# An encoder block on one core: later modulation columns with the weights as the moving operand, and loads for weight sums placed behind the raw weights of their step

## The chip, the cores and the metric

The kernel runs on one core of one Trainium2 chip. The metric is the device time of an execution in microseconds; lower is better.

## The reference

One encoder layer serves two request groups, a prompt of 2048 tokens and a sample of 512, with 1024 channels. A conditioning vector per group gives six vectors of 1024 numbers that modulate the layer. All is float32.

```python
mod = silu(c) @ w_ada + b_ada              # w_ada: 1024 x 6144, c: 2 rows in all
shift1, scale1, gate1, shift2, scale2, gate2 = split(mod, 6)
h = rmsnorm(x, g_mix_norm) * (1 + scale1) + shift1
z = h @ w_in
y_f = fourier_mixer(z[..., :512])          # 2-D DFT, then per-head maps
y_s = s5_mixer(z[..., 512:])               # bidirectional state space, GELU, GLU
x = x + gate1 * (concat(rmsnorm(y_f), rmsnorm(y_s)) @ w_out)
h = rmsnorm(x, g_mlp_norm) * (1 + scale2) + shift2
ff = square(relu(h @ w_mlp_in + b_mlp_in)) @ w_mlp_out + b_mlp_out
return rmsnorm(x + gate2 * ff, g_final)
```

## The kernel before

Activations lie with channels on the partitions and tokens along the free dimension. The modulation vectors are kept the same way, as `mod`, 128 partitions by 48 columns by 2 groups: column j holds 128 of the 6144 numbers. Products that need more than one pass are split: each operand into a high part (a cast, `wh`, `th`) on ScalarE and a low part (the rest, `wl`) on VectorE, and `mm3` (lines 229 to 231) issues three matmuls, high by high, high by low, low by high.

The stages in order of time: the input projection with the first sixteen modulation columns (`ada1`, line 705: the two conditioning rows stationary, 512 weight columns moving, then four small transposes at line 710); a stage from about 345 to 690 us in which blocks of the state-space scan (`psV` at L350, `psY` at L382), the Fourier mixer (`px`, `pyc`, `pys`) and its output (`pof`) share TensorE with the 32 later modulation columns; the gated units and the output projection (`pgate`, `pval`, `pout`), to about 1020 us; and the MLP.

The later columns: `ada(j)` (line 681) multiplies one 128-column piece of `w_ada` in eight matmuls. The weights are stationary, the two columns of `cs` (the activated conditioning) move, and the result has channels on partitions; VectorE adds the bias (L688). `ada_slot` calls it once in each of 32 slots between pieces of the scan. Its weights, 512 KB a column, are loaded on the SP queue into two buffers named `wa` (`AB = 2`): the load for column j+2 is issued behind the matmuls of column j, whose buffer it takes.

The MLP works by a scheme with seven products for eight, so it needs sums of weight quarters. `precombine` (line 1247) makes a sixteenth of one weight's sums: four loads of 256 KB on SP (L1258), four additions on GpSimd (L1263), four stores of 256 KB on ScalarE's DMA queue (L1264) to a scratch in DRAM, `wS`. Twenty of the 32 pieces are made beside the output projection; the last twelve, all for the second MLP weight, are made in the first 60 steps of the MLP, in a buffer (`big4`) that those steps don't need yet, with room for three pieces at a time. A step is twelve matmuls against 128 x 512 weights. Two steps share a load of raw weights (`wr`, L1394), and in the first third of the MLP the low parts are also stored for later (`wL`, L1408). The first block's input is scaled by VectorE and ScalarE (`h2`, L1324 and L1325) before its first product.

The order on every engine is set by the scheduler of the framework, which places instructions by a model of time; each engine and each DMA queue then runs its own in that order. `tc.issue_after(ins)` makes the instructions of a block that run on the engine of `ins` come behind it there.

Of the kernel before, what the change touches and what calls it, by code (L numbers as in the profile page):

```python
# [26 lines left out]
AB = 2  # L27
# [532 lines left out]
class Net:  # L560
# [3 lines left out]
    def run(self):  # L564
        tc, nc, A = self.tc, self.nc, self.A
        with ExitStack() as es:
            self.cp = es.enter_context(tc.tile_pool(name="cp", bufs=1))
            dp = self.dp = es.enter_context(tc.tile_pool(name="dp", bufs=1, space=DRAM))
            self.pst, self.side = None, False
            self.pr = es.enter_context(tc.tile_pool(name="psr", bufs=1, space=PSUM))  # L570
            self.banks(7)
            es.callback(lambda: self.pst.close())
            self.uD = dp.tile([512, 8, 320], F32, name="uD")
            self.yD = dp.tile([512, 8, 320], F32, name="yD")
            self.fD = dp.tile([4, 128, NT], F32, name="fD")
            nb = 32 // NQ
            self.sD = [dp.tile([nb, 128] + sh + [NQ, 128], F32, name="s%d" % i) for i, sh in enumerate(([2], [2], []))]
            self.sD.append(dp.tile([nb, 128, 3, NQ, 40], F32, name="s3"))
            self.zD = dp.tile([4, 5, 128, 258], F32, name="zD")
            self.pD = dp.tile([8, 128, NT], F32, name="pD")  # L580
            self.rD = dp.tile([128, NT], F32, name="rD")
            self.x1D = dp.tile([8, 128, NT], F32, name="x1D")
            self.wS = [dp.tile([4, 8, 128, 1024], F32, name="wS%d" % i) for i in range(2)]

            self.wL = dp.tile([112, 128, 1024], F32, name="wL")
            self.consts()
            def pool(name, side=None):
                st = ExitStack()
                return st, st.enter_context(tc.tile_pool(name=name, bufs=1, side=side))
            spps, spp = pool("spp", "right")  # L590
            fes, fe = pool("fe", "right")
            self.Ze = [fe.tile([96, n], F32R, name="Ze%d" % n) for n in (352, 256)]
            self.aj, self.wa = 16, {}
            self.pcs = [(w, c) for w in range(2) for c in range(16)]
            P = self.mix_in(spp)
            sas, sa = pool("ssa", "right")
            sps, sp = pool("ssm", "right")
            S = Ssm(self, P, sa, sp, self.uD.rearrange("(g h) t n -> (h t) g n", g=32), self.yD.rearrange("(g h) t n -> (h t) g n", g=32), *self.sD)
            self.ada_open(sa, 48)
            gen = self.beside()  # L600
            self.pull(gen, U0)
            bl = []
            for q in range(nb + 2):
                if q < nb:
                    bl.append(S.lead(q))
                    self.slot(gen)
                if 1 <= q <= nb:
                    S.step2(bl[q - 1])
                if q >= 2:
                    self.slot(gen)  # L610
                    S.step3(bl[q - 2])
                    self.slot(gen)
                if q < nb:
                    S.step1(bl[q])
                    self.slot(gen)
            self.pull(gen, 1000)
            self.banks(7)
            sps.close()
            sas.close()
            fes.close()  # L620
            spps.close()
            xb = es.enter_context(tc.tile_pool(name="xb", bufs=1))
            self.x0 = xb.tile([128, 16, 428], F32, name="x0")
            self.mws = es
            self.mix_out()
            self.mlp()
# [53 lines left out]

    def ada(self, j):
        nc = self.nc
        v3 = lambda n: self.v[n].unsqueeze(2).broadcast_to([128, 8, 2])
        ps = self.ps([128, 2], "pa")
        w = self.wa.pop(j)
        for k in range(8):
            nc.tensor.matmul(ps, w[:, k], self.cs[:, k], start=k == 0, stop=k == 7)  # L687
        nc.vector.tensor_scalar(self.mod[:, j], ps, self.v["b_ada"][:, j:j + 1], None, op0=ALU.add)  # L688
        if j == 39:
            nc.vector.scalar_tensor_tensor(self.gs2, self.mod[:, 32:40], 1.0, v3("g_mlp_norm"), op0=ALU.add, op1=ALU.mult)  # L690
        if j == 47:
            nc.vector.tensor_scalar(self.ng2, self.mod[:, 40:48], -1.0, None, op0=ALU.mult)
            nc.vector.tensor_tensor(self.gb2, self.mod[:, 40:48], v3("b_mlp_out"), op=ALU.mult)
# [21 lines left out]
    def ada_slot(self):  # L715
        j = self.aj
        if j < self.aend:
            self.ada(j)
            if j + AB < self.aend:
                self.ada_load(self.adp, j + AB, AB)  # L720
            self.aj += 1

    def ada_open(self, tp, end):
# [542 lines left out]
    def mlp(self):  # L1266
        tc, nc, A = self.tc, self.nc, self.A
# [11 lines left out]
        with tc.tile_pool(name="mp1", bufs=1, side="right") as t1, tc.tile_pool(name="mp", bufs=1, side="right") as tp:  # L1279
# [5 lines left out]
            def big(bl, role):  # L1285
                return ring[bl["slots"][role]][:, :, :bl["n"]]
# [100 lines left out]
            raws, los = {}, {}  # L1387
            trail = lambda st: self.wL[(st["i"] % (2 * PH)) // 2].rearrange("p (a b) -> p a b", a=2)

            def raw(i):  # L1390
                st = steps[i]
                w = A["w%d" % st["ph"]] if st["kind"] == "raw" else self.wS[st["ph"] - 1]
                raws[i] = mw.tile([128, 2, 512], F32, tag="wr", name="wr", bufs=3)
                nc.sync.dma_start(raws[i].rearrange("p a b -> p (a b)"), w[st["j"], st["m"] // 2])  # L1394
                los[i] = mw.tile([128, 2, 512], F32R, tag="wl", name="wl", bufs=3)
                if st["bl"] is not blocks[0]:
                    nc.sync.dma_start(los[i].bitcast(F32), trail(st))
# [109 lines left out]
            def pre2(c):  # L1507
                if c == 0:
                    bl = blocks[0]
                    bl["sc"] = big(bl, "21").rearrange("p a b -> p (a b)")  # L1510
                t = blocks[0]["sc"]
                self.precombine(lambda n, i: t[:, 512 * (i + 4 * (c % 3)):512 * (i + 4 * (c % 3)) + 512])
            for c in range(len(self.pcs)):
                at(P0 + (60 - P0) * c // len(self.pcs), pre2, c)
            for st in steps:
# [5 lines left out]
            for i in range(len(steps) + 24):  # L1521
                for f, a in hooks.get(i, ()):
                    f(*a)
                if i >= len(steps):
                    continue
                for j in ([0, 1, 2] if i == 0 else [i + LW]):
                    if j < len(steps):
                        if j % 2 == 0 and j not in raws:
                            raw(j)
                        weights(j)  # L1530
                if (i + 4) % 2 == 0 and i + 4 < len(steps) and i + 4 not in raws:
                    raw(i + 4)
                (mm_in if steps[i]["ph"] == 1 else mm_out)(steps[i])
# [15 lines left out]
```

## Time and profile before

| | us |
|---|---|
| median of 3 runs | 2659.03 |
| lowest and highest | 2655.82, 2665.93 |
| the profiled execution | 2665.03 |
| its span, first to last instruction | 2663.3 |
| TensorE busy | 2530.6 (95%) |
| weight loads on TensorE | 2285.1 (86%) |
| VectorE busy | 1683.9 (63%) |
| ScalarE busy | 1293.1 (49%) |
| GpSimd busy | 478.7 (18%) |
| mean granted TensorE clock | 0.954 |
| DMA moved | 627 MB, 236 GB/s in the mean |

The busy time of TensorE includes matmuls that run at the lower of its two clocks, and the profile models the ends of matmuls, so a busy engine can still be slower than it might be; the granted clock of a stretch (1 is 2.4 GHz, 0.5 is 1.2 GHz) tells how much. In the trace an f32 matmul shows as two records and one on split operands as one. A chain of waits is followed back from the last instruction to what released each step.

### The profile page before, as it was taken

The numbers are of one execution on the slowest core, as the hardware profiler recorded it, in microseconds if no ns is written. First come the engines' busy times: TensorE is split into PE (matmuls) and PEld (weight loads), VectorE is DVE, ScalarE is ACT, GpSimd is POOL, SyncE is SP. The second block draws the span as 40 slices with busy tenths as digits, with TensorE's granted clock in tenths as the row PEclk, the third lists the DMA queues.
The fourth block names the chain that finished last, engine by engine and source line by source line (L and its number), as shares of the span: only waits on it lengthen the run. The fifth ranks groups of instructions, "written<-read, shape, count | busy, mean of one in ns | idle before, by whom it ended". The sixth has DMA issues, their size and how long they took to land.

```text
span 2663.3 us, 35333 instructions
## 1 busy us (share of the span) xinstructions
PE 2530.6 (95%) x12643; PEld 2285.1 (86%) x12643; DVE 1683.9 (63%) x2775; ACT 1293.1 (49%) x2267; POOL 478.7 (18%) x406
## 2 busy tenths in 40 slices
PE   6889999999989999799999999999999999999997
PEld 2778878778767779689999999999999999999997
DVE  7888778776638866758867973354456433634454
ACT  2643466564534425525544557355445573654443
POOL 4410010000346430940400002004000020130000
PEclk8789988879999999899999999999999999999998
DMA  8644476455678978997666777676667766766664
GB/s 293 205 146 113 141 246 214 163 171 184 206 274 268 308 253 288 339 365 277 233 218 216 276 257 251 228 273 230 226 230 276 248 243 226 274 226 227 226 222 163
DMA packets 279040, 627.31 MB, mean 236 GB/s; under 512 B 66512, under 2 KB 110608, under 8 KB 277072
## 3 DMA queue, kind: packets, MB, share of 16 engines
q1 hardware_dynamic: 238416, 549.13, 60.3%
q10 hardware_dynamic: 34096, 61.32, 6.2%
q0 software_dynamic: 6352, 14.60, 1.7%
q8 instruction: 100, 1.64, 0.3%
q14 instruction: 76, 0.62, 0.1%
HBM read 469.10 MB, written 155.85 MB: 235 GB/s over the span
## 4 chain that ended last, share of the span: by engine, by line
PE 68%; DVE 12%; DMA 10%; ACT 4%; issue 4%; POOL 2%; ACTq 0%; SPq 0%; DVEq 0%; POOLq 0%
PE acc L231 9%; PE acc L230 9%; PE acc L229 9%; PE pf L231 8%; PE pf L230 8%; PE pf L229 8%; PE pa L687 2%; PE psY L382 2%; PE psV L350 1%; DMA xq<-in_xq 1%; POOL q L1263 1%; DMA wS<-q 1%; DMA q<-in_w 1%; DVE wl L1406 1%; PE pof L229 1%
## 5 line engine op out<-in xcount | busy, mean ns | idle before, releaser
L1404 ACT CAST wh<-wr 128x512 fp32r<-128x512 f32 x672 | 413.4, 620 | 689.3 <-PE acc L230 342.7
L229 PE MATMUL pf<-th,wh 128*128 128x426 f32 (+1 forms) x1344 | 483.2, 360 | 19.7 <-ACT wh L1404 19.6
L230 PE MATMUL pf<-th,wh 128*128 128x426 f32 (+1 forms) x1344 | 482.2, 359 | 1.0 <-DVE th L1357 1.0
L231 PE MATMUL pf<-th,wl 128*128 128x426 f32 (+1 forms) x1344 | 477.3, 359 | 5.2 <-DVE wl L1406 5.1
L230 PE MATMUL acc<-th,wh 128*128 128x426 f32 (+1 forms) x1344 | 478.4, 357 | 0.3 <-DVE th L1357 0.3
L229 PE MATMUL acc<-th,wh 128*128 128x426 f32 (+1 forms) x1344 | 474.5, 357 | 0.0
L231 PE MATMUL acc<-th,wl 128*128 128x426 f32 (+1 forms) x1344 | 466.9, 357 | 2.1 <-DVE wl L1406 2.0
L1424 DVE TENSOR_TENSOR big<-big,pf 128x426 f32<-128x426 f32 (+1 forms) x320 | 185.1, 596 | 237.2 <-PE pf L231 191.6
L1357 DVE TENSOR_TENSOR th<-big,th 128x1704 fp32r<-128x1704 f32 (+1 forms) x82 | 158.8, 1936 | 201.8 <-ACT th L1356 201.5
L229 PEld LDWEIGHTS pf<-th,wh 128*128 128x128 f32 x1344 | 254.3, 189 | 32.8 <-ACT wh L1404 23.4
L231 PEld LDWEIGHTS pf<-th,wl 128*128 128x128 f32 x1344 | 254.3, 189 | 18.0 <-DVE wl L1406 9.1
L230 PEld LDWEIGHTS pf<-th,wh 128*128 128x128 f32 x1344 | 254.7, 190 | 10.1 <-DVE th L1357 1.4
L231 PEld LDWEIGHTS acc<-th,wl 128*128 128x128 f32 x1344 | 253.2, 189 | 11.2 <-DVE wl L1406 2.8
L230 PEld LDWEIGHTS acc<-th,wh 128*128 128x128 f32 x1344 | 252.5, 188 | 9.5 <-DVE th L1357 1.1
L229 PEld LDWEIGHTS acc<-th,wh 128*128 128x128 f32 x1344 | 252.9, 188 | 9.0
L750 POOL TENSOR_TENSOR r<-r,mh 128x4 f32<-128x4 f32 (+3 forms) x32 | 35.3, 1109 | 1145.1 <-DVE r L749 1145.1
L1431 POOL TENSOR_TENSOR big<-big 128x426 f32<-128x426 f32 (+1 forms) x128 | 142.6, 1118 | 493.4 <-ACT big L1430 490.1
L1406 DVE TENSOR_TENSOR wl<-wr,wh 128x512 fp32r<-128x512 f32 x224 | 174.9, 799 | 62.6 <-ACT wh L1404 62.1
L1263 POOL TENSOR_TENSOR q<-q,q 128x512 f32<-128x512 f32 x80 | 138.4, 1730 | 79.6 <-DMA q<-in_w 57.4
L1356 ACT CAST th<-big 128x1704 fp32r<-128x1704 f32 (+1 forms) x82 | 132.5, 1616 | 0.7 <-PE acc L231 0.7
L1357 DVE TENSOR_TENSOR th<-x,th 128x1704 fp32r<-128x1704 f32 (+1 forms) x23 | 47.5, 2066 | 69.3 <-ACT th L1356 69.3
L1430 ACT ACTIVATE big<-big 128x426 f32<-128x426 f32 (+1 forms) x128 | 71.3, 559 | 38.7 <-DVE big L1424 35.5
(444 smaller groups left out, 4453.4 us busy)
## 6 DMA issues: line engine op xcount, KB each, us to landing
wl<-wL SPq DMA_DIRECT2D x224, 512.0 KB, 3.5
wr<-wS SPq DMA_DIRECT2D x192, 512.0 KB, 4.5
wr<-in_w SPq DMA_DIRECT2D x144, 512.0 KB, 4.4
wL<-wl SPq DMA_DIRECT2D x112, 512.0 KB, 3.4
wa<-in_w_ada SPq DMA_DIRECT2D x48, 512.0 KB, 4.7
q<-in_w SPq DMA_DIRECT2D x80, 256.0 KB, 4.3
wS<-q ACTq DMA_DIRECT2D x80, 256.0 KB, 3.7
big<-x1D SPq DMA_DIRECT2D x8, 1704.0 KB, 7.8
```

The lines of the kernel that those rows point to most:

```text
L229: nc.tensor.matmul(out, l[0], r[0], start=start, stop=False)
L230: nc.tensor.matmul(out, l[0], r[1], start=False, stop=False)
L231: nc.tensor.matmul(out, l[1], r[0], start=False, stop=stop)
L382: nc.tensor.matmul(py, m, x[:, j], start=i == 0, stop=i == 2)
L1263: e.tensor_tensor(o, x, y, op=op)
L1356: nc.scalar.copy(th[0], src)
L1357: return th, v.tensor_tensor(th[1], src, th[0].bitcast(F32), op=ALU.subtract)
L1404: nc.scalar.copy(hi, r)
L1406: v.tensor_tensor(lo, r, hi.bitcast(F32), op=ALU.subtract)
L1424: v.tensor_tensor(f[q], f[q], ps, op=op)
L1430: nc.scalar.activation(f[q], f[q], AF.Relu)
L1431: nc.gpsimd.tensor_tensor(f[q], f[q], f[q], op=ALU.mult)
```

## The change

The later columns take the form of the first sixteen: `cs` is stationary (two columns), the 128 weight columns move, and the result is a 2 x 128 row. ScalarE copies it into the front of the weights' own buffer; TensorE transposes it to 128 x 2, and VectorE adds the bias as before. The transpose and the addition of a column are issued one slot later, in `ada_turn`, behind the matmuls of the next column. Since the row lies in the weights' buffer, the buffer comes free with the transpose; the load of column j+1 is then issued in slot j, behind the transpose of column j-1. In the MLP, the loads of a weight sum are placed behind the last raw-weight load that was issued before them.

```diff
     def ada(self, j):
-        ps = self.ps([128, 2], "pa")
+        ps = self.ps([2, 128], "pa")
         w = self.wa.pop(j)
         for k in range(8):
-            nc.tensor.matmul(ps, w[:, k], self.cs[:, k], start=k == 0, stop=k == 7)
+            nc.tensor.matmul(ps, self.cs[:, k], w[:, k], start=k == 0, stop=k == 7)
+        r = w[:2, 0]
+        nc.scalar.copy(r, ps)
+        self.ada_turn()
+        self.turn = (j, r)
+
+    def ada_turn(self):
+        if not self.turn:
+            return
+        (j, r), self.turn = self.turn, None
+        ps = self.ps([128, 2], "pat")
+        nc.tensor.transpose(ps, r, self.ident[:2, :2])
         nc.vector.tensor_scalar(self.mod[:, j], ps, self.v["b_ada"][:, j:j + 1], None, op0=ALU.add)
...
             self.ada(j)
-            if j + AB < self.aend:
-                self.ada_load(self.adp, j + AB, AB)
+            if 16 < j <= self.aend - AB:
+                self.ada_load(self.adp, j + AB - 1, AB)
...
-                nc.sync.dma_start(raws[i].rearrange("p a b -> p (a b)"), w[st["j"], st["m"] // 2])
+                self.wload = nc.sync.dma_start(raws[i].rearrange("p a b -> p (a b)"), w[st["j"], st["m"] // 2])
...
-                self.precombine(lambda n, i: t[:, 512 * (i + 4 * (c % 3)):512 * (i + 4 * (c % 3)) + 512])
+                with tc.issue_after(self.wload.ins):
+                    self.precombine(lambda n, i: t[:, 512 * (i + 4 * (c % 3)):512 * (i + 4 * (c % 3)) + 512])
```

TensorE among the later columns, between the Fourier mixer and the scan's outputs, before the change (`pa` are the columns, two of them, 36 and 37, in the first row and two in the last; `psY` are the scan's outputs):

```order
L687 MATMUL pa<-cs,wa 128x2 x16
L382 MATMUL psY<-un,Th 128x320
L382 MATMUL psY<-S,O 128x320 x2
L382 MATMUL psY<-un,Th 128x320
L382 MATMUL psY<-S,O 128x320 x2
L382 MATMUL psY<-un,Th 128x320
L382 MATMUL psY<-S,O 128x320 x2
L382 MATMUL psY<-un,Th 128x320
L382 MATMUL psY<-S,O 128x320 x2
L687 MATMUL pa<-cs,wa 128x2 x16
```

and at a like place with the change (columns 32, 33 and 34; `pat` is a transpose, buffer numbers tell which weights):

```order
L687 MATMUL pa_5101<-wa_5018,cs_93 2x128 x8
L702 MATMUL pat_5111<-ident_84,wa_4947 128x2
L687 MATMUL pa_5156<-wa_5114,cs_93 2x128 x8
L702 MATMUL pat_5166<-ident_84,wa_5018 128x2
L382 MATMUL psY_5236<-un_4370,Th_4423 128x320
L382 MATMUL psY_5236<-S_5227,O_4421 128x320
...
L687 MATMUL pa_5257<-wa_5169,cs_93 2x128 x8
L702 MATMUL pat_5267<-ident_84,wa_5114 128x2
```

The eight matmuls of a column now come as one piece with a transpose of the column before behind them; `wa_5114` takes the buffer of `wa_4947`, so the second row's transpose stands directly ahead of the matmuls that need the load issued behind it.

SP's queue in the first steps of the MLP, before (`wr` raw weights, `wL` stores of low parts, `big4` the loads of sums):

```order
L1394 DMA wr_9490<-in_w1 128x1024
L1408 DMA wL_79<-wl_9416 128x1024
L1394 DMA wr_9542<-in_w1 128x1024
L1258 DMA big4_9177<-in_w2 128x512 x12
L1408 DMA wL_79<-wl_9454 128x1024
L1408 DMA wL_79<-wl_9492 128x1024
L1394 DMA wr_9580<-in_w1 128x1024
L1394 DMA wr_9638<-in_w1 128x1024
```

and with the change, beginning with the fifth raw load:

```order
L1409 DMA wr_9422<-in_w1 128x1024
L1273 DMA big4_9273<-in_w2 128x512 x4
L1423 DMA wL_79<-wl_9336 128x1024
L1409 DMA wr_9460<-in_w1 128x1024
L1273 DMA big4_9273<-in_w2 128x512 x2
L1423 DMA wL_79<-wl_9374 128x1024
L1273 DMA big4_9273<-in_w2 128x512 x2
L1409 DMA wr_9510<-in_w1 128x1024
```

The loads of sums stood twelve in a row behind the tenth raw load; now they come one piece (four loads) at a time from the fifth on.

VectorE at the entry of the MLP, before (`xo` are the output projection's additions, `x` the scaling of the MLP's input, `wl` low weights, `th` the input's low part):

```order
L1324 SCALAR_TENSOR_TENSOR x_6810<-x_6810,gs_98,rb 128x428 x14
L1229 TENSOR_TENSOR ss<-ss,sq 128x512
L1224 SCALAR_TENSOR_TENSOR xo<-pout,mod,xo 128x512
L1220 SCALAR_TENSOR_TENSOR xo<-pf,mod,xo 128x512
L1324 SCALAR_TENSOR_TENSOR x_6810<-x_6810,gs_98,rb 128x428 x2
L1406 TENSOR_TENSOR wl<-wr,wh 128x512 x4
L1220 SCALAR_TENSOR_TENSOR xo<-pf,mod,xo 128x512
L1224 SCALAR_TENSOR_TENSOR xo<-pout,mod,xo 128x512
L1357 TENSOR_TENSOR th_9179<-x_6810,th_9178 128x1712
```

and with the change:

```order
L1239 SCALAR_TENSOR_TENSOR xo<-pout,mod,xo 128x512
L1339 SCALAR_TENSOR_TENSOR x_6906<-x_6906,gs_98,rb 128x428 x15
L1244 TENSOR_TENSOR ss<-ss,sq 128x512
L1339 SCALAR_TENSOR_TENSOR x_6906<-x_6906,gs_98,rb 128x428
L1421 TENSOR_TENSOR wl<-wr,wh 128x512 x4
L764 TENSOR_SCALAR r<-pn 128x4
L1372 TENSOR_TENSOR th_9275<-x_6906,th_9274 128x1712
```

Before, several of the projection's additions stood behind the scaling; now the first row is the last of them, and the whole scaling follows.

## Rows read from the trace of the kernel before

**Rows 1.** Windows by stage: stretch and length, busy us (instructions) per engine, clock, DMA share, GB/s.

```profile
345.00:690.00 345.00, 337.91 (x1649) 276.90 (x1648) 264.18 (x695) 193.91 (x449) 11.50 (x16) 0.86 0.59 193
1020.00:1200.00 180.00, 154.90 (x753) 142.12 (x753) 113.64 (x130) 79.36 (x139) 96.24 (x66) 0.94 0.94 340
1200.00:2663.00 1463.00, 1444.76 (x7440) 1394.01 (x7439) 802.73 (x1042) 736.40 (x1131) 147.18 (x140) 0.99 0.68 239
```

**Rows 2.** Chain of waits from 345 to 690 us, shares by line.

```profile
by line: PE pa L687 12.5%; PE psY L382 12.4%; PE psV L350 9.8%; PE pof L230 5.5%; PE pof L229 5.5%; PE pof L231 5.5%; issue 4.1%; PE px L229 3.7%; PE px L231 3.6%; PE px L230 3.6%; DMA fD<-yF 3.1%; DMA raw<-in_w_out 2.3%; PE pc L999 1.6%; A
```

**Rows 3.** Timeline of TensorE: start, length in us, line, tiles, shapes, records.

```profile
345.35 6.83 PE L687 MATMUL pa<-cs,wa 128*128 128x2 f32 x32
...
616.61 1.84 PE L687 MATMUL pa<-cs,wa 128*128 128x2 f32 x16
...
627.47 1.86 PE L382 MATMUL psY<-un,Th 128*128 128x320 f32 x6
```

**Rows 4.** Windows of L687 alone, 340 to 660 us: their sum.

```profile
sum 320.00, PE 71.05 PEld 72.84; mean PE 11.84 PEld 12.14
```

**Rows 5.** Windows of 6 us, columns as in rows 1.

```profile
336.00:342.00 6.00, 2.38 (x8) 0.89 (x6) 1.29 (x4) 5.89 (x21) 4.78 (x8) 1.00 0.87 250
342.00:348.00 6.00, 5.44 (x20) 4.07 (x18) 3.70 (x9) 5.80 (x19) 0.00 (x0) 0.51 1.07 373
...
408.00:414.00 6.00, 6.00 (x32) 5.15 (x32) 5.55 (x17) 3.01 (x14) 1.50 (x3) 0.69 1.13 356
```

**Rows 6.** Timeline of TensorE among the first sixteen columns.

```profile
39.51 3.59 PE L705 MATMUL pa<-wa,cs 128*2 128x512 f32 x8
...
51.47 0.41 PE L710 MATMUL pat<-ident,ar 2*128 2x2 f32 x4 [2.27 <-ACT ar L707]
```

**Rows 7.** Windows of 4 us among the first sixteen columns, columns as in rows 1.

```profile
28.00:32.00 4.00, 4.00 (x6) 0.60 (x5) 3.50 (x26) 1.15 (x2) 0.00 (x0) 0.57 1.03 350
...
40.00:44.00 4.00, 3.10 (x8) 0.44 (x6) 3.97 (x11) 0.77 (x1) 2.91 (x2) 1.00 0.48 140
```

**Rows 8.** Tile wa, whole span: ns min/median/max, first and last start.

```profile
L705 PEld LDWEIGHTS pa<-wa,cs x64: 80/85/129, 5.7 to 48.2; 128*2 128x2 f32 x64
```

**Rows 9.** Tile wa, 340 to 660 us: its loads, issue to landing.

```profile
DMA to landing us min/median/max: 3.1/3.9/11.1
```

**Rows 10.** Windows in the first steps of the MLP, columns as in rows 1.

```profile
1170.00:1180.00 10.00, 7.92 (x40) 6.80 (x39) 7.76 (x8) 2.28 (x4) 5.82 (x5) 1.00 1.05 411
1057.00:1187.00 130.00, 105.94 (x490) 94.82 (x489) 86.05 (x86) 57.30 (x98) 94.23 (x64) 0.92 0.96 352
1130.00:1187.00 57.00, 52.63 (x256) 46.98 (x256) 35.13 (x44) 13.46 (x22) 30.73 (x22) 1.00 1.02 379
1187.00:1250.00 63.00, 63.00 (x325) 60.74 (x324) 43.51 (x73) 32.03 (x53) 0.00 (x0) 1.00 0.77 272
```

**Rows 11.** Timeline of SP's queue: the first loads of sums in the MLP.

```profile
1056.99 6.70 SPq L1258 DMA_DIRECT2D big<-in_w  x12
```

**Rows 12.** Timeline of TensorE in the MLP: waits in brackets with their releaser.

```profile
1021.05 0.46 PE L230 MATMUL pf<-th,wh 128*128 128x428 f32 x1 [1.03 <-DVE th L1357]
...
1081.77 0.72 PE L229 MATMUL pf<-th,wh 128*128 128x428 f32 x1 [9.92 <-ACT wh L1404]
```

**Rows 13.** DMA issues from 1057 to 1187 us: count, KB each, median us to landing.

```profile
big<-in_w SPq DMA_DIRECT2D x48, 256.0 KB, 6.2
wS<-big ACTq DMA_DIRECT2D x48, 256.0 KB, 6.1
```

**Rows 14.** Groups of VectorE, 1000 to 1060 us: busy us, mean ns, idle before.

```profile
L1406 DVE TENSOR_TENSOR wl<-wr,wh 128x512 fp32r<-128x512 f32 x16 | 10.7, 686 | 7.8 <-ACT wh L1404 7.8
L1324 DVE SCALAR_TENSOR_TENSOR x<-x,gs,rb 128x428 f32<-128x428 f32 x16 | 9.4, 656 | 1.1 <-DMA rb<-rD 1.1
...
L1224 DVE SCALAR_TENSOR_TENSOR xo<-pout,mod,xo 128x512 f32<-128x512 f32 x10 | 7.4, 744 | 0.1
...
L1357 DVE TENSOR_TENSOR th<-x,th 128x1712 fp32r<-128x1712 f32 x2 | 3.9, 1932 | 3.9 <-ACT th L1356 3.9
```

More of the change, by code (lines that the diff above doesn't have):

```diff
@@ L592, in run @@
             self.Ze = [fe.tile([96, n], F32R, name="Ze%d" % n) for n in (352, 256)]
-            self.aj, self.wa = 16, {}
+            self.aj, self.wa, self.turn = 16, {}, None
             self.pcs = [(w, c) for w in range(2) for c in range(16)]
@@ L682, in ada @@
         nc = self.nc
-        v3 = lambda n: self.v[n].unsqueeze(2).broadcast_to([128, 8, 2])
-        ps = self.ps([128, 2], "pa")
+        ps = self.ps([2, 128], "pa")
         w = self.wa.pop(j)
         for k in range(8):
-            nc.tensor.matmul(ps, w[:, k], self.cs[:, k], start=k == 0, stop=k == 7)
+            nc.tensor.matmul(ps, self.cs[:, k], w[:, k], start=k == 0, stop=k == 7)
+        r = w[:2, 0]
+        nc.scalar.copy(r, ps)
+        self.ada_turn()
+        self.turn = (j, r)
+    def ada_turn(self):
+        nc = self.nc
+        if not self.turn:
+            return
+        (j, r), self.turn = self.turn, None
+        v3 = lambda n: self.v[n].unsqueeze(2).broadcast_to([128, 8, 2])
+        ps = self.ps([128, 2], "pat")
+        nc.tensor.transpose(ps, r, self.ident[:2, :2])
         nc.vector.tensor_scalar(self.mod[:, j], ps, self.v["b_ada"][:, j:j + 1], None, op0=ALU.add)
```

## Prediction

> **What bounds the kernel now.** I read the busy time by stage first [rows 1]. From 1200 us on TensorE is busy 1444.8 of 1463 us; the change issues the same instructions there, so nothing of it is costed. From 690 to 1020 only their order moves (zero, give or take 5 us). Two stages are touched: 345 to 690 us, in which the 32 later modulation columns run among the state-space and Fourier work, and 1020 to 1200 us, the entry of the MLP with the last twelve weight sums. In the first, TensorE is busy 337.9 of 345 us, but at a granted clock of 0.86. The chain of waits there [rows 2] has the columns' matmuls (L687) as its largest line, 12.5%; the shares that the row shows for TensorE add up to 64%, the rest is VectorE, ScalarE and DMA. So I count a microsecond saved on TensorE there at 0.64.
>
> Next the columns themselves [rows 3]: 32 of their records take 6.83 us in one place, 213 ns each, and 16 take 1.84 us in another, 115 ns; a record is half an f32 matmul. The first pace is that of the lower clock (1.2 GHz), the second of the higher (2.4 GHz). Then slices of 6 us [rows 5]: between 408 and 414 us the clock stands at 0.69, right behind 26 of these records that began at 407.6. Of the twelve falls between 345 and 660 us that I find in such slices, ten come right behind a run of them; the others follow a wait, as that of 336 to 342 us, where TensorE was busy 2.38 of 6 us and the next slice ran at 0.51. A long matmul against two moving columns is an engine that loads weights and streams next to nothing.
>
> **The columns, term by term, on TensorE.** Their own time: 512 records fill 71.05 us [rows 4]. In the new form (two stationary columns, 128 moving) they look like L705, the first sixteen columns, which already run so with 512 moving: 8 records in 3.59 us [rows 6], 449 ns, and a quarter of that is 112 ns. 512 records of 112 ns are 57.3 us: 14 less. The price could be more, if the load of the two columns, 80 to 85 ns [rows 8], were not hidden behind so short a matmul: at worst 512 x 80 ns, 41 us. I take it as hidden, since the old form hides a load of 128 columns well enough to issue a record every 115 ns [rows 3].
>
> The Trainium skill, "TensorE: Matmul & The Clock Gate", section "LDWEIGHTS (loading the stationary operand)", has the load grow with the stationary columns alone: about 107 ns for 128, under 2 ns for two. The first agrees with the old pace; the second does not with the 80 ns of [rows 8]. By the page the 41 us of the worst case would be under 1 us.
>
> 32 new transposes: four take 0.41 us [rows 6], 0.10 us each, together 3.3 us more. The 32 copies on ScalarE and the moved VectorE additions are a few hundred ns each, and nothing waits for these columns before the output projection, 300 us later; zero, unless ScalarE (194 of 345 us busy [rows 1]) is late with one and a transpose waits.
>
> The clock: 0.86 over 345 us means 48 us of full-speed work lost [rows 1]; 14 of it is the columns' own, counted above, so 34 fell on their neighbours. Does the new form hold the clock? L705 says so [rows 7]: at 28 to 32 us it begins at the low clock behind a wait (0.57), and at 40 to 44 us eight of its records, alone on the engine, run at 1.00. By ten falls of twelve I give three quarters of the 34 back: 26 us less.
>
> The loads: before, the load for column j+2 is issued behind matmul j, now that for j+1 behind the transpose of j-1, which stands behind matmul j. Half the lead is gone; the chain per column is transpose, issue on SP, landing, next matmul, and all TensorE work behind that matmul waits with it. A landing took 3.9 us in the median and 11.1 at most [rows 9]; with the issue and the semaphores about 4.4. I counted the TensorE work that the new order leaves between a transpose and the matmul that needs the buffer, at the full-clock spacings of the trace (six records of 320 f32 columns in 1.86 us [rows 3], and the like): eight of thirty pairs hold less than 4.4 us (0.0, 1.4, 2.6, 3.0, 3.1, 3.6, 3.7, 3.8). The shortfalls add up to 14 us. Where TensorE would have waited for something else anyway they cost nothing; if every load took 11 us they would be some 130.
>
> Sum on TensorE: -14 + 3 - 26 + 14 = -23 us, at 0.64 about **-14 us**.
>
> **The MLP's entry.** Before, twelve sum loads were issued in a row at 1057 us [rows 11], the raw weights of the next steps behind them, and the ScalarE queue had seven stores of sums ahead of the next weight split; TensorE then sat 9.92 us [rows 12]. From 1057 to 1187 us it ran 490 matmuls [rows 10]; at the later pace of 63 us for 325 these are 95 us, so 35 were lost. Now the sums come four loads at a time behind a raw weight, from about the fifth step to the 58th. The transfers don't shrink: 48 loads and 48 stores of 256 KB [rows 13] are 25.2 MB, and 53 steps bring 0.52 MB each of raw and low weights, together 53 MB. At 379 GB/s, the rate of the saturated stretch [rows 10], that is 140 us, against 123.5 us of TensorE work (53 x 2.33): 16.5 us lost. At 411 GB/s, the best 10 us of it, 5.5; at the mean of 352 GB/s 27.
>
> Against that stands the order on VectorE at the entry. Before, 14 of 16 scalings of the first block (L1324) stood ahead of the last additions of the output projection, and TensorE waited 1.03 us at its first products [rows 12]. Now all sixteen come behind the last addition. Counted from the last projection matmul: an addition and a further sum (0.74 each, as L1224), 16 x 0.656, four low weights of 0.69, and 1.93 for the low part of the input [rows 14]: 16.7 us, and TensorE has under 1 us to do meanwhile. That is 15 us more than before. Sum: -35 + 16.5 + 15 = **-4 us** (-15 to +8).
>
> **Total.** -14 - 4 = -18 us. The profiled execution took 2665.03 us, so 2647; it lay 6 us above the median of 2659.03, which makes the forecast **2641 us**.
>
> **Rivals.** *Both in full*: the pairs are hidden by other waits, the clock stays up throughout (own -14, neighbours -34, transposes +3, at 0.64: -28), and the entry is filled as before with transfers at 411 GB/s (-30): 2601 us. For it: in the stage TensorE already waits for others at places, where a load can hide; against: the order as it stands. *Clock not held*: two stationary columns with 128 moving do not count as L705's 512 do. Then only transposes and shortfalls are left, +17 at 0.64, with -4: 2666 us, no change by the 0.5% (13 us) that a measurement can tell. Against it is [rows 7]. *Another engine takes over*: VectorE is busy 264 of the 345 us [rows 1] and the chain runs through its scans; if they set the pace, the stage gives nothing back: 2655 us, no change either. *The loads come late* (the slower side): with SP in order, and the load behind a transpose, a landing of 8.5 us instead of 3.9 (it happens where DMA is above 1.0 busy, as at 342 to 348 us [rows 5]) makes the shortfalls 77 us, and waits of that length pull the clock down, as behind 336 to 342 us, say 10 us more; -37 + 77 + 10 = 50, at 0.64 +32, with -4: 2687 us. It decides from a landing of about 7.5 us on. For it: one slot of lead is all there is; against: the median.
>
> On the last the Trainium skill, same page, section "Loop structure matters more than you think", warns of matmuls that each wait for a DMA, since they then run cold. The row of 336 to 348 us agrees, with 0.51 behind the wait.
>
> **How the numbers follow.** Forecast 0.46, both in full 0.17, clock not held 0.09, another engine 0.14, loads late 0.14. The forecast's own spread (2629 to 2655) lies about two thirds beyond 0.5% (under 2646): faster 0.32 + 0.17 = 0.49; within 0.5% 0.14 + 0.09 + 0.14 = 0.37; slower 0.14. The range, 2608 to 2668, leaves out the late loads and the far end of the good case.
>
> **What would show it.** Right: the granted clock from 345 us to the end of the stage above 0.93, L687 records spaced near 110 ns, waits of TensorE for the tile wa of some 14 us in all, a wait of about 15 us ahead of the first MLP matmuls, and no wait of 10 us later. Wrong: a clock still near 0.86 (clock not held); landings of wa above 7 us; a stage as long as before with TensorE waiting for VectorE; or an entry as tight as before.

## Result: the changed kernel and its profile

The changed kernel takes 2689.22 us in the median (2687.33 to 2690.04), the kernel before 2661.17 beside it (2655.82 to 2665.93): a ratio of 1.0105, 95% interval 1.0083 to 1.0127. It is slower by 28 us where 2641 was forecast. All readings below are of the profiled executions: 2689.74 us (span 2687.9) after, 2665.03 (span 2663.3) before.

The first table puts marks of both traces side by side: the starts of the first and last records of a kind, in us. `pof` is the Fourier output projection, `pout` the output projection, `pf` the first MLP product, of which twelve records are a step. The last column is the kernel k1 of the last experiment, which differs from the changed one in a PSUM tile only (a buffer that matmuls write to).

| | before | after | k1 |
|---|---|---|---|
| first later column | 345.3 | 344.0 | 342.8 |
| last later column | 656.3 | 707.5 | 654.8 |
| its transpose | none | 712.7 | 660.1 |
| first load of a weight sum | 680.3 | 733.7 | 682.6 |
| last `pof` | 755.2 | 758.1 | 735.5 |
| last `pout` | 1019.4 | 1033.0 | 999.8 |
| first `pf` | 1019.7 | 1056.2 | 1004.8 |
| step 60 of the MLP | 1199.8 | 1220.2 | 1183.6 |

Taken as differences, after against before: columns to last `pof` +4.2, output projection +10.7, from there to the first MLP product +22.9, the first 60 steps -16.1, from there to the last matmul of the MLP +5.9 (1444.0 us became 1449.9; other kernels whose code there is the old one show up to 1448.7, so this is mostly scatter). The sum is 27.6; ahead of the columns and behind the last matmul 3.0 us were saved, which leaves the 24.6 us between the two spans.

The stage from 345 to 690 us, which [rows 1] showed for the kernel before, in a view by stretch (busy us of each engine, the granted clock, the share and rate of the DMA engines):

```profile
core 0: us, PE busy (x) PEld busy (x) DVE busy (x) ACT busy (x) POOL busy (x), PEclk, DMA share, GB/s
345.00:690.00 345.00, 312.21 (x1614) 230.31 (x1612) 259.50 (x685) 188.28 (x463) 13.51 (x16) 0.93 0.54 175
...
1033.00:1056.00 23.00, 2.25 (x10) 1.78 (x8) 19.14 (x32) 13.21 (x23) 1.75 (x2) 0.59 0.81 272
1056.00:1220.00 164.00, 149.24 (x728) 138.03 (x729) 99.22 (x108) 75.14 (x132) 96.05 (x64) 0.97 0.94 338
```

The clock rose from 0.86 to 0.93, as the forecast wanted. But TensorE is now idle for 33 of the 345 us instead of 7, and it got less done: 1614 records against 1649. And a stretch of 23 us has appeared ahead of the MLP in which it does almost nothing. What TensorE waited for, first between 340 and 760 us, then between 760 and 1221 (us in total, times, longest):

```profile
PE pa L687 <- DMA wa<-in_w_ada: 18.1, 6, 4.4
...
PE pn L751 <- DVE ss L1244: 22.1, 4, 18.2
PE pf L231 <- DVE wl L1421: 11.8, 10, 4.0
...
PE pf L229 <- ACT wh L1419: 2.7, 3, 1.8
```

The first is the wait for the columns' loads, absent before. The second is the new wait at the MLP's entry, 18.2 of the 22.1 us. The last two answer to [rows 12]; in the kernel before they were, between 1010 and 1200 us:

```profile
PE pf L229 <- ACT wh L1404: 19.6, 5, 9.9
PE pf L231 <- DVE wl L1406: 4.3, 5, 2.4
```

The wait of 9.92 us is gone, and the two together fell from 23.9 to 14.5 us: over half of the -16.1. The granted clock there is 0.97 for 0.94.

The first table has one more thing that no wait shows: the later columns end 51 us later, and so does the scan (its last record begins at 705.5 for 654.4). Behind them stands the SP queue. From 706 us on (start, duration, what it loads or stores):

```profile
706.46 0.37 SPq L384 DMA_DIRECT2D yD<-y  x1
710.93 0.32 SPq L1158 DMA_DIRECT2D pD<-of  x1
712.98 0.33 SPq L1184 DMA_DIRECT2D rawo<-in_w_glu  x1
714.80 6.35 SPq L1158 DMA_DIRECT2D pD<-of  x3
722.68 0.33 SPq L1184 DMA_DIRECT2D rawo<-in_w_glu  x1
723.36 8.03 SPq L1158 DMA_DIRECT2D pD<-of  x3
732.43 1.24 SPq L1197 DMA_DIRECT2D y<-yD  x2
733.72 2.03 SPq L1273 DMA_DIRECT2D q<-in_w  x3
```

The gated units' weights (`rawo`) are loaded once the columns are through, then the scan's outputs (`y`), then the first weight sum (`q`). Before, the same row began at 656.6 and reached the sum at 680.3:

```profile
656.59 0.83 SPq L1169 DMA_DIRECT2D rawo<-in_w_glu  x1
...
680.31 1.93 SPq L1258 DMA_DIRECT2D q<-in_w  x3
```

The 20 sums beside the output projection then take some 292 us in both kernels (80 loads from 680.3 to 972.8, and from 733.7 to 1024.6). So here their last loads stand ahead of the loads for the last output additions (`xo`, `pf`), and the MLP's opening loads come after these:

```profile
1021.26 3.68 SPq L1273 DMA_DIRECT2D q<-in_w  x4
...
1034.24 0.33 SPq L1231 DMA_DIRECT2D xo<-in_xT  x1
1035.17 0.33 SPq L1233 DMA_DIRECT2D pf<-pD  x1
1039.23 0.98 SPq L1333 DMA_DIRECT2D rb<-rD  x2
1040.26 1.54 SPq L1409 DMA_DIRECT2D wr<-in_w  x3
```

In the kernel before, `rb` (the row that scales the MLP's first block) was issued at 999.6 us. Here its load waited 3.6 us in the queue for the stores of the last sum, landed at 1042.1, and VectorE's scalings follow:

```profile
1042.23 8.71 DVE L1339 SCALAR_TENSOR_TENSOR x<-x,gs,rb 128x428 f32<-128x428 f32 x15 [0.19 <-DMA x1D<-xo]
```

### The profile page after: what moved, and what is told of

It reads as the page before. It is cut to its first block, busy times and chain, and to the rows that moved or that the text cites. A ratio compares the mean times of both kernels' runs of the same rounds, so it can differ in the third digit from the quotient of the medians.

```text
span 2687.9 us, 35457 instructions
## 1 busy us (share of the span) xinstructions
PE 2519.8 (94%) x12675; PEld 2248.4 (84%) x12675; DVE 1696.6 (63%) x2775; ACT 1298.8 (48%) x2299; POOL 470.9 (18%) x406
## 4 chain that ended last, share of the span: by engine, by line
PE 65%; DVE 14%; DMA 11%; ACT 4%; issue 3%; POOL 1%; SPq 0%; ACTq 0%; DVEq 0%; POOLq 0%
PE acc L231 9%; PE acc L230 9%; PE acc L229 9%; PE pf L231 8%; PE pf L229 8%; PE pf L230 8%; PE pa L687 2%; PE psY L382 2%; DMA wa<-in_w_ada 2%; DMA q<-in_w 1%; DVE wl L1421 1%; DMA xq<-in_xq 1%; DMA wS<-q 1%; DVE ys L1221 1%; PE psV L350 1%
## 5 line engine op out<-in xcount | busy, mean ns | idle before, releaser
L231 PEld LDWEIGHTS pf<-th,wl 128*128 128x128 f32 x1344 | 253.6, 189 | 27.2 <-DVE wl L1421 18.5
L1278 POOL TENSOR_TENSOR q<-q,q 128x512 f32<-128x512 f32 x80 | 123.4, 1543 | 152.4 <-DMA q<-in_w 83.8
L687 PE MATMUL pa<-wa,cs 128*2 128x128 f32 x512 | 72.6, 302 | 18.6 <-DMA wa<-in_w_ada 18.1
```

What stands on the lines that cost most here:

```text
L231: nc.tensor.matmul(out, l[1], r[0], start=False, stop=stop)
L687: nc.tensor.matmul(ps, self.cs[:, k], w[:, k], start=k == 0, stop=k == 7)
L1278: e.tensor_tensor(o, x, y, op=op)
```

## Experiments

Four questions came up one after the other: which part of the change costs time; whether it is the short lead of the loads; what a late end of the columns costs; and what makes them late. Medians are given with the ratio to the kernel before in the same session, with its 95% interval.

**Which part.** e1 leaves the sums' loads queued as before, e2 leaves the columns as before:

```diff
-                with tc.issue_after(self.wload.ins):
-                    self.precombine(...)
+                self.precombine(...)
```

> The columns' part of the change alone; the sums' loads are queued as before. Theory A (the columns' part brings the loss, the other part a gain): last fourier projection at about 758 us as in the changed kernel, a wait of about 20 us of TensorE for VectorE's sum of squares at the MLP's entry, first MLP matmul at about 1056, then the first 60 steps take about 180 us as before instead of the changed kernel's 164: about 2700 us, some 10 to 16 us above the changed kernel. Theory B (the queued sums bring the loss): no wait at the entry, 2655 to 2665 us.

> The sums' part alone: the columns as before, the sums' loads behind their step's raw weights. Theory A: all up to 1020 us as before, first MLP matmul at about 1020, the first 60 MLP steps in about 165 us instead of 180: about 2645 us. Theory B: the spread sums cost time, 2675 us or more.

e1 took 2701.16 us, 1.0165 (1.0143 to 1.0188); e2 2659.63, 1.0009 (0.9995 to 1.0023). So theory A holds for e1 in every number: last `pof` at 759.6 us, first `pf` at 1052.5, a wait of 20.7 us ahead of it, 179.6 us for 60 steps. For e2 it fails: nothing was gained. Its SP queue still held the first twelve loads of sums in a row, and TensorE waited as before:

```profile
PE pf L229 <- ACT wh L1404: 17.3, 3, 9.9
```

The edge that was added, sums behind a raw weight, was met in that order as it stood. Only in the order that comes with late columns did the loads spread out; there they brought the 12 us between the medians of e1 and the changed kernel.

**The lead of the loads.** Theory A also said that the shorter lead eats what the clock gives. e5 is the kernel before with the short lead; e4 is the changed kernel with the long one, in that each column group is transposed behind the other work of its own slot:

```diff
         nc.scalar.copy(r, ps)
-        self.ada_turn()
         self.turn = (j, r)
...
         nc.vector.tensor_scalar(self.mod[:, j], ...)
+        if j + AB < self.aend:
+            self.ada_load(self.adp, j + AB, AB)
...
         self.ada_slot()
         self.pull(gen, 1)
+        self.ada_turn()
```

> The kernel before, columns still as the stationary operand, with one edit: each load of a column group goes out one slot ahead instead of two, as in the changed kernel. Theory A: waits for wa of 10 to 20 us appear where the kernel before has none, the clock stays at about 0.86, the last fourier projection comes 8 to 14 us later (763 to 769), and the time is about 2670. Theory C: waits under 4 us, 2661.

> The changed kernel, but each column group is transposed behind the other work of its own slot, so that its buffer is free earlier and the next load goes out nearly two slots ahead, as before. Theory A (the short lead eats what the clock gives back): waits for wa fall from 18 us to under 6, the granted clock of 345 to 690 us stays at 0.92 or above, the last fourier projection comes at 740 to 746 instead of 758; the wait at the MLP's entry stays near 20 us, so the time is about 2675. Theory C (the lead is not it, the loads are slow through contention or the clock is spent elsewhere): waits for wa over 12 us, last fourier projection within 4 us of 758, about 2689.

e5 took 2658.63 us, 0.9998 (0.9985 to 1.0010), with no wait for these loads: a short lead costs nothing in the old order. e4 took 2667.11, 1.0036 (1.0022 to 1.0049): no waits for `wa` (9.0 us for ScalarE's copies instead), last `pof` at 731.6, columns' end at 687.4. So theory A is half right. In the changed order the lead, with the transpose's new place, is worth some 20 us (22 between the medians, 18 by the ratios); but the same short lead is harmless in another order. Lead and order count together.

The two orders differ plainly in one count. Of the 480 `pof` matmuls, 120 start ahead of the scan's last record in the kernel before, 279 in the changed one, 300 in e4. That the scheduler fills with them what it takes for gaps in the scan and the columns is likely, but not shown.

**What a late end costs.** Theory D, later named G, reads the SP rows above: the sums begin some 25 us behind the last column, their chain of 292 us follows, and the MLP's opening waits for its end. g1 makes the chain longer in the kernel before (`PCG = 24` for 20):

> The kernel before, columns untouched, with 24 instead of 20 weight sums beside the output projection (and 8 instead of 12 in the MLP). Theory D (the end of the chain of sums gates the MLP's opening): sums of about 14.6 us each from 680 on end near 1030, the first MLP matmul comes at 1045 to 1060 instead of 1020 with a wait of 15 to 30 us in front, although the columns' code, clock and last Fourier projection are those of before; after it the first 60 MLP steps are up to 20 us shorter, since 4 sums are gone from there: 2660 to 2680 us. Against it: no wait at the entry, 2640 to 2655 us.

2684.82 us, 1.0088 (1.0061 to 1.0115). The last sum loads came at 1018.1, the first `pf` at 1048.5 instead of 1020, with the columns as they were. The time is above the range expected, since the first 60 steps fell to 166.8 us only. i1 makes the end late instead, with the columns' code untouched: the three scan steps in each slot get a lower priority in the scheduler.

```diff
...
-                    S.step1(bl[q])
+                    with self.first(-150):
+                        S.step1(bl[q])
```

> The kernel before with the three scan steps of each slot at a lower priority for the scheduler; the columns are untouched. It puts 254 instead of 120 of the 480 matmuls of the Fourier output projection ahead of the scan's and columns' last. Theory G (the sums begin about 25 us behind the last column group, since their buffers lie in the memory of the columns' weights, and their chain gates the MLP): columns end near 690 instead of 656, first sum load near 714, chain of 292 us to about 1006, a wait of 10 to 25 us at the MLP's entry, first MLP matmul at 1035 to 1045: 2665 to 2685 us, with the granted clock and the columns' form of before. Against it (the columns' new form costs in itself): 2661 and no wait at the entry.

2688.85 us, 1.0118 (1.0101 to 1.0134), above the range expected and the time of the changed kernel. 254 `pof` ahead, columns' end at 691.4, first sum at 714.9, first `pf` at 1035.4, step 60 at 1220.8. Its stretch from 345 to 690 us and its wait at the entry:

```profile
345.00:690.00 345.00, 337.88 (x1627) 280.29 (x1626) 259.28 (x688) 188.04 (x443) 12.56 (x16) 0.85 0.55 179
...
PE pn L739 <- DVE ss L1232: 19.0, 1, 19.0
```

The columns to the last `pof` take 409.8 us, as before. So the columns' new form is not needed for the loss; that they and the scan end late is enough. In all twenty kernels of this document the first load of a sum is issued 21 to 25 us behind the last record of the columns (with their transposes) and the scan, whichever ends later.

Is it the wait at the entry that costs? With two buffers for each quarter of a sum the chain is shorter (`precombine(tp, 2)` for `precombine(tp, 1)`, one line): in the kernel before (h0), the changed one (h1), e4 (h2), and e4 with 24 sums (h3).

> The kernel before with two buffers instead of one for each of the four weight quarters that a sum beside the output projection loads, so that the next sum's loads need not wait for the last one's stores. Theory G (the chain of 20 sums, some 14.6 us each with one buffer, begins when the scan ends, and the MLP's first tiles lie in its memory; in the kernel before it ends 47 us ahead of the first MLP matmul and decides nothing): the chain ends earlier than 973 us, the rest as before, 2652 to 2664 us. Against it: 10 us or more faster.

> The changed kernel with that same edit alone. Theory G: the last sum's loads come well ahead of 1000 us instead of at 1025, the first MLP matmul follows the last output matmul (1020 to 1033) within 5 us instead of 23, but the first 60 MLP steps take about 180 us again instead of 164, since PE comes to them earlier than their weights and sums allow: about 2675 us, 10 to 16 below the changed kernel. Against it: the wait at the entry stays and the time stays at 2689.

> The run with each column group transposed in its own slot (2667 us), with that same edit. Theory G: last Fourier projection near 732, last output matmul near 1000, no wait of 33 us at the MLP's entry, first 60 steps in about 180 us: about 2647 us. Against it: 2667.

> As the run before it, with 24 instead of 20 sums beside the output projection and 8 in the MLP. Theory G: with two buffers a sum takes some 10 to 12 us of the chain, so 24 end by 1000 and the entry stays without a long wait, while the first 60 MLP steps lose 4 sums of their transfers: 160 to 170 us instead of 180, about 2632 to 2642 us. If the chain gates again (ends behind 1010): 2655 or more.

h0: 2664.82, 1.0013 (1.0001 to 1.0025). h1: 2692.04, 1.0119 (1.0100 to 1.0137). h2: 2667.19, 1.0017 (1.0004 to 1.0031). h3: 2681.19, 1.0079 (1.0060 to 1.0099). In h1 and h2 the wait at the entry vanished, from 23 and 33 us to 0.3 each, as theory G said; yet neither kernel is faster than the one it was made from. The output projection grew instead, from 275 to 290 us in h1 and from 274 to 292 in h2, and in h1 the first steps went back to waiting for their weights:

```profile
PE pf L229 <- ACT wh L1419: 16.2, 5, 8.0
```

So the wait is a symptom that moves about. What stays is the time from the first load of a sum to step 60: 486 us in the changed kernel, 492 in h1, 485 in e4, 482 in h2, 506 in i1, whatever the order in between. Where the sums begin early the time is longer (520 us in the kernel before, 501 in k1), so there it is not what sets step 60. In that stretch of the changed kernel the DMA engines were busy by 0.88 of the time, in that of the kernel before by 0.85:

```profile
DMA packets 88630, 146.59 MB, mean 302 GB/s; under 512 B 28054, under 2 KB 30614, under 8 KB 88344
```

That transfers pace the stretch where it is short agrees with this, and with h3, where 24 sums and two buffers brought a wait of 29.3 us back; no run took the transfers themselves away, so it is argued and not shown. What these runs show is that the loss comes with a late start of the sums and does not go with the entry's wait.

**What makes columns and scan late.** The changed kernel takes two PSUM tiles for each column where the old one took one: `pa` for the result, `pat` for the transpose. Both come in turn from the four buffers that the scan's `psV` and `psY` rotate through. Theory D, later H: the extra turn holds the scan up in the scheduler's model. f2 takes the transposes' tile from the three buffers of the side work instead, in the changed kernel and with the long lead; f3 takes both tiles from there; i2, i3 and i4 give the first group five buffers and the side work two (`NB = 5`), in the changed kernel, in e4 and in the kernel before.

> The changed kernel with one edit: the 32 transposes take their PSUM tile from the three buffers of the side work instead of the four that the scan and the columns share; the short lead of the loads stays. Theory D (the transposes' tile takes a turn in the scan's four PSUM buffers; so the order puts 279 instead of 120 of the 480 matmuls of the Fourier output projection ahead of the scan's end, the sums begin 50 us later and their chain of about 292 us ends behind the output projection): columns end near 655 instead of 707, first load of a sum near 680 instead of 734, last near 972, first MLP matmul right behind the last output matmul, no wait for wa over 3 us in total as with the short lead alone, granted clock of the stage 0.92 or more, last Fourier projection near 735: about 2640 us. Theory A (the short lead of the loads eats the gain): the waits for wa stay near 18 us, the last Fourier projection at 750 or later; 2660 or more.

> As the run with the transposes' PSUM tile among the side work's buffers, and each column group transposed within its own slot so that its load goes out two slots ahead. Theory D: within 4 us of that run, about 2637 to 2640, since the lead is not what cost time. Theory A: 15 to 20 us faster than that run.

> As the run before it, and the columns' own accumulator too among the side work's three PSUM buffers, so the scan has its four to itself. Theory D: the scan ends still earlier (no matmul of the Fourier output projection stands ahead of its last), the sums begin at 640 to 670 and end before 970, no wait at the MLP's entry; the side work has less room, so 2630 to 2650. If the scan's end decides nothing, the time is that of the run before it.

> The changed kernel with five PSUM buffers for scan, columns and transposes, and two instead of three for the side work. Theory H (the transposes' tile takes a turn among the scan's buffers, and that makes the scan and the columns late): the order then has 123 of the 480 matmuls ahead of the scan's last, columns end by 670 instead of 707, sums begin by 695, no wait at the entry; with the short lead's waits of 10 to 18 us for wa left: 2655 to 2672 us. If the buffers aren't it, columns end at 690 or later and the time is 2685 or more.

> The run with each column group transposed in its own slot (2667 us), with the same five and two PSUM buffers. Theory H: no matmul of the Fourier output projection ahead of the scan's last, columns end at 620 to 650, first sum load 25 us later, no wait at the entry, last Fourier projection still near 732 to 745: 2635 to 2650 us. If not: 2665.

> The kernel before with five and two PSUM buffers, the control for the two runs before it. The scan and the columns end earlier (order: none of the 480 matmuls ahead), but the sums' chain did not gate here and the clock of the stage stays near 0.86, so theory G and H expect no gain beyond 8 us: 2652 to 2664 us. If the five buffers are what helps, 2645 or less.

| | `pof` ahead | columns' end | last `pof` | first sum | step 60 | median, ratio (interval) |
|---|---|---|---|---|---|---|
| f2 | 120 | 687 | 781 | 710 | 1229 | 2695.91, 1.0122 (1.0099-1.0145) |
| f2, long lead | 120 | 681 | 777 | 703 | 1225 | 2688.51, 1.0100 (1.0076-1.0123) |
| f3 | 0 | 664 | 759 | 689 | 1208 | 2678.29, 1.0064 (1.0042-1.0085) |
| i2 | 123 | 691 | 797 | 717 | 1232 | 2700.61, 1.0156 (1.0142-1.0171) |
| i3 | 0 | 625 | 781 | 657 | 1217 | 2683.24, 1.0100 (1.0083-1.0119) |
| i4 | 0 | 615 | 818 | 638 | 1267 | 2730.43, 1.0258 (1.0236-1.0280) |

None gave the time that was expected. The order answered (120 and 0 for 279), so the tile does move it, but the side work, which had to share or lost buffers, got slower by more: the last `pof` came at 759 to 818 us, also in the kernel before (i4). Where the columns end early and the Fourier projection late, the sums are early and the time is lost all the same; that TensorE's own work behind the projection then sets step 60 is likely but not shown. f3 settled one detail: its scan ended at 604.8 and its columns at 663.7,

```profile
L382 PE MATMUL psY<-S,O x128: 432/432/900, 403.9 to 604.8; 128*128 128x320 f32 x128
...
656.41 0.40 SPq L680 DMA_DIRECT2D wa<-in_w_ada  x1
661.77 0.32 SPq L1158 DMA_DIRECT2D pD<-of  x1
667.18 0.33 SPq L1184 DMA_DIRECT2D rawo<-in_w_glu  x1
```

and the gated units' weights were loaded right behind the columns (their last transpose began at 666.9), not behind the scan. So the columns alone can hold up the next stage's loads. The scan can as well: in i1, where its last record (692.9) came behind the last column, the same load went out at 693.3.

k1 and k2 take no buffer from anyone: result and transpose of a column lie in one tile, in the changed kernel (k1) and with the long lead (k2).

```diff
-        ps = self.ps([2, 128], "pa")
+        ps = self.ps([128, 256], "pa")
+        pt, ps = ps[:, 128:130], ps[:2, :128]
...
-        ps = self.ps([128, 2], "pat")
         nc.tensor.transpose(pt, r, self.ident[:2, :2])
```

> The changed kernel, with result and transposes of a column group in one PSUM tile, so that each group again takes one turn among the scan's four buffers, as before, though for longer. The order has 186 instead of 279 of the 480 matmuls of the Fourier output projection ahead of the scan's last. Theory H (the second tile makes the scan late): columns end at 680 to 690 instead of 707, sums begin 25 us behind that, and the time falls by as much as the sums come earlier: 2665 to 2675 us. If only the number of matmuls ahead moves and the stage grows by new waits, as with the side work's buffers: last Fourier projection at 770 or later, 2689 or more.

> The same, with each group transposed in its own slot and the load two slots ahead. Order: 200 instead of 300 matmuls ahead. Theory H: columns end near 665 instead of 687, last Fourier projection still near 732 to 740, first sum load near 690, step 60 of the MLP some 485 to 500 us later: 2645 to 2660 us. If the stage grows by new waits: 2667 or more.

k1 took 2658.80 us, 0.9985 (0.9972 to 0.9997), 30 us less than the changed kernel and 6 less than the theory had; k2 2652.29, 0.9962 (0.9948 to 0.9977), faster than both kernels, though by 0.4% only against the one before. 186 and 200 `pof` stand ahead, the last columns come at 654.8 and 654.7 and their transposes at 660.1 and 659.1, the sums begin at 682.6 and 681.5, and the last `pof` comes at 735.5 and 733.4. In k1, between 345 and 690 us and further on:

```profile
345.00:690.00 345.00, 328.99 (x1735) 243.80 (x1733) 264.82 (x698) 203.37 (x486) 12.81 (x16) 0.98 0.60 194
690.00:1005.00 315.00, 288.82 (x1278) 230.91 (x1278) 233.84 (x296) 131.91 (x206) 138.29 (x90) 0.97 0.83 278
1005.00:1184.00 179.00, 155.22 (x739) 142.66 (x739) 115.64 (x125) 78.26 (x136) 96.07 (x65) 0.92 0.92 329
...
PE pa L688 <- DMA wa<-in_w_ada: 3.2, 1, 3.2
```

The waits for `wa` fell from 18.1 to 3.2 us though k1 keeps the short lead, the clock stands at 0.98, and 1735 records were done where the kernel before did 1649. So the second PSUM tile is what made the change a loss: the lateness, most of the waits and most of the entry's gap (5.0 us are left of 23.2) go with it. How the tile makes the scheduler run the columns late is read from the counts alone. k1's 60 steps take 178.8 us, since the sums' loads come in a row again; with columns in time the second part of the change brings nothing, as in e2. One caution on k1's profile: it is of the fastest of eleven executions, 7 us under their median, and that of the kernel before lies 4 us above the median beside k1. Of the 13.5 us between the two spans the medians keep 2; no trace shows where the others lose the rest.

The Trainium skill, "Perfetto Trace Analysis", section "Identifying Performance Opportunities", says that gaps which repeat on the engine that should be busy can mean too little room in SBUF or PSUM for the next tile. The trace of the changed kernel agrees only in part: the shortage showed as six waits for a DMA and a wait 300 us later, and no row named PSUM.

## Why the prediction was wrong, step by step

Forecast was -18 us, found is +24.6 between the spans. Of the 42.6 us between them 18.2 lie in the stage from 345 us, 10.7 from there to the last `pout`, 10.8 at the MLP's entry and 2.9 in the rest.

*The clock: right.* Forecast over 0.93, found 0.93, and 0.98 in k1 with fewer waits.

*The columns' own time: no gain in the changed kernel, right in sign only in k1 and k2.* 71.05 us was to become 57.3; it was 72.6 in the changed kernel (its records run in part at the lower clock), 64.9 in k1, 63.5 in k2. A quarter of L705's record, 112 ns, was near: at the higher clock sixteen of the new records take 1.91 us, 119 ns each. But sixteen of the old took 1.84 [rows 3], so the whole gain is the clock's. The transposes took 7.2 us, not 3.3.

*The shortfalls of the loads: right in size (14 forecast, 18.1 found), half right in reason.* They were counted from the order and explained by the halved lead. With the long lead (e4) they are gone; but e5 has the short lead without such waits, and k1 with 3.2 us of them. It takes the changed kernel's order as well, and that goes with the second tile.

*The transposes at 3.3 us and "From 690 to 1020 only their order moves (zero, give or take 5 us)": the step that failed.* The transposes were priced by TensorE's time alone; that each takes one more tile from the buffers of the scan was put at nothing, and no reason was given. With it the columns and the scan end 51 us later, and what follows them costs 10.7 us up to the last `pout` and most of the 22.9 at the entry; without it (k1) the change costs nothing. The new order was read for the gaps between a transpose and its load; not asked was how far other work had moved past the columns, and what starts behind them. The count of `pof` ahead, 279 for 120, was in the order to be read, and the 24 us from last column to first sum and the 292 us of the chain in the trace of the kernel before. An estimate from these: 159 more matmuls, 0.23 us apart, put the columns' end some 36 us later (51 were found), and the last sum's loads to about 1009 us, where `rb` can no longer be issued at 999.6 us.

*The stage's sum, -14 us:* +4.2 in the changed kernel. In k1, which has no second tile, the first column to the last `pof` took 392.7 us against 409.9, or -17, and in k2 389.2; five other kernels with the old columns and four buffers took 407 to 410. That fits the factor of 0.64: at 0.98 the clock gives back 41 of the 48 us, and less 7 for the transposes and 3 for the waits these are 31, at 0.64 some 20.

*The entry, -4 us:* 15 us more were forecast ahead of the first product and 22.9 found, 18.2 of them in one wait. The order on VectorE was read rightly: all sixteen scalings come behind the last addition. But the additions behind the last projection matmul took 9.0 us (1033.0 to 1042.0) where 1.5 was counted: three of them were still to come, and their last loads were issued at 1034.2 and 1035.2. And that `rb` would land only at 1042.1, behind the last sum, was not seen. The 60 steps behind it gained 16.1 where 18.5 was forecast, yet only in the late order (e2, k1: at most 1.4). Together +6.8.

*The rivals.* "The loads come late" gave 2687 us, close to what came, by a mechanism that was not there: instead of 7.5 us or more, a landing of `wa` took 3.7 in the median in the changed kernel's stage, and the stage's clock rose. So the nearness is luck. The rival that came true, a later start of the next stage, was not among them.

## What to carry over

A new temporary, however small, takes a turn in whatever rotation of buffers it is allocated from; ask who else rotates there before costing its work, and where it can share a tile that is held anyway. When a schedule moves, read first which work now ends later and whose buffers lie in its memory: a chain that begins there can set the time of a stage 300 us on. A wait that appears at a stage's entry may be only where a late chain shows; remove it and see whether the time follows.

## What the runs showed of the hardware

The matmuls with two stationary columns and 128 moving held the clock in this case, although each is preceded by a weight load that the trace of the changed kernel shows at 80 to 85 ns:

```profile
L687 PEld LDWEIGHTS pa<-wa,cs x512: 80/85/130, 344.0 to 707.4; 128*2 128x2 f32 x171
L687 PE MATMUL pa<-wa,cs x512: 269/273/422, 344.0 to 707.5; 128*2 128x128 f32 x171
```

(ns, least, median, most; first and last start.) Sixteen in a row took 1.91 us, 119 ns each, at a granted clock of 1.00, so that load lay beside the matmuls. In k1 the clock falls three times between 345 and 690 us, at 398, 541 and 558 us; each time TensorE had just waited, for 1.4, 3.2 and 1.2 us, and none of the falls stands behind a run of columns. The old form held 128 stationary and two moving columns, took 115 ns each at the higher clock [rows 3], and the clock fell to 0.69 right behind it [rows 5]. So the two forms were issued at nearly the same pace, and the clock fell behind runs of the old one and, in k1, not behind runs of the new one.
